# A hybrid token mixer with an MLP behind it: loads of x on another queue, squares in PSUM, and a second norm in fewer steps

## The chip, the cores and the metric

The program runs on one core of a Trainium2 chip. The metric is the device time of one execution in microseconds (us). A core has TensorE (PE, matrix products), VectorE (DVE), ScalarE (ACT), GpSimd (POOL) and SyncE (SP, which here only issues transfers). Each engine works through its own list of instructions in order and waits at the head of that list until the semaphores of the instruction are there. ACT, POOL and SP also issue DMA transfers from their lists.

## The reference

One layer: a mixer of three head groups, an output projection, then a squared-ReLU MLP and a last norm. What the change touches starts at the output projection.

```
def rmsnorm(x, g):
    y = x * lax.rsqrt(jnp.mean(x * x, axis=-1, keepdims=True) + NORM_EPS)
    return y * g
def modulate(x, g, shift, scale):
    return rmsnorm(x, g) * (1 + scale) + shift
def sq_relu_mlp(h, w1, w2):
    return jnp.square(jax.nn.relu(h @ w1)) @ w2

# x (1, 1024, 1024), w_out (1024, 1024), w1 (1024, 4096), w2 (4096, 1024), all float32
x = x + g1 * (concat(hyena, gla, gdn) @ w_out)
x = x + g2 * sq_relu_mlp(modulate(x, norm2_g, sh2, sc2), w1, w2)
out = rmsnorm(x, final_norm_g)
```

## The kernel before

Everything is held transposed: features on the 128 partitions, tokens along the row. x is eight tiles `x1_0` to `x1_7` of 128 features by 1024 tokens. The token axis has two halves, c=0 and c=1.

The nine products behind the mixer (w_out; then four groups of 1024 hidden features, each with a w1 and a w2 product) all go through `stage`. A stage computes a 1024x1024x1024 product as seven products i = 1..7 of 512-blocks (a Strassen scheme) in an order O1, O2 or O3. One product i has four groups p of output features, each with four contraction tiles k and three matmuls (high by high, high by low, low by high: a float32 value is split into two reduced parts, line 292, `split`), so 48 matmuls of 512 columns; a stage has 336. The moving side of product i is four tiles `T` (`sums`, made one product ahead), the stationary side is a tile `S` for each p, cut out of a loaded weight tile `wr0` to `wr3`. ACT makes the high part of both (line 295), DVE the low part of `T` and POOL the low part of `S` (line 255).

Sums of weight blocks are made by the transfers themselves: `weights` loads a block from SP's list (line 1493) and adds others to it by accumulating transfers from POOL's list (line 1487), by the plan of the order (`PLANS`). Four rooms hold five such tiles of a stage in turn.

Products add into eight PSUM banks (`psb`). `take` is called when a group p of a product is done: in w_out and w2 it is `adder`, which adds the bank to x1 (DVE, line 263) and, where a feature tile is then complete, squares it (ACT) and adds the square to `acc` (DVE). In w1 it is `up`, which makes the squared ReLU into tiles `ar`.

`w_out` loads x1 at its start (line 1681). `norm2(c)` runs inside a stage, after a group named by a constant: `NORM_AT = (3, 1)` puts the norm of c=0 behind group p=1 of product i=3 in w_out, `NORM1_AT = (1, 3)` that of c=1 behind p=3 of i=1 in the first w1. `rstd` sums `acc` over features on PE (`ones`), takes the root on ACT and the reciprocal on DVE, and spreads the result over the partitions on PE (`ident`). Then h = x1 * rstd (DVE, for c=0 half of it on POOL) and h * A2 + shift (ACT). For c=1 the first four tiles of h are at last replaced by the difference of second and first half, which the first w1 (order O2) uses.

The text's order is not the lists' order: the framework orders the instructions of each engine by priority (text position, lowered inside `sooner`) and a simulated timeline. Transfers of SP and ACT share eight completion semaphores in turn, so a transfer also waits until the one that had its semaphore before has landed.

Of the kernel before, what the change touches and what calls it, by code (L numbers as in the profile page):

```python
# [184 lines left out]
URGENT = 100000  # L185
# [4 lines left out]
MODN = 2  # L190
ORD0=range(8)
ORD1 = (0, 4, 1, 5, 2, 6, 3, 7)
POOL0 = (4, 5, 6, 7)
POOL1 = ()
FPOOL = ((0, 2, 5), (0, 2, 5))
# [6 lines left out]
LAST_AT = (1, 1)  # L202
NORM_AT = (3, 1)
NORM1_AT = (1, 3)
FINAL_AT = (4, 1)
# [9 lines left out]
class Build:  # L215
# [1292 lines left out]

    def stage(self, src, order, moving, take, after=None, last=None, first=None):

# [22 lines left out]
        for n, i in enumerate(order):  # L1533
            begin_w(n + 2)
            if last and n == 6:

                s = [w(i, p) for p in range(4)]
                for j in range(2):
                    c = slice(256 * j, 256 * j + 256)
                    for p in range(4):  # L1540
                        ps, _ = bank(i, p)
                        for k in range(4):
                            ks = slice(128 * k, 128 * k + 128)
                            self.mm3(ps[:, c], (s[p][:, 0, ks], s[p][:, 1, ks]), (T[i][k][:, 0, c], T[i][k][:, 1, c]), False, k == 3, True)
                        take(i, p, ps, c)
                        if after and j == 0 and (i, p) == after[:2]:
                            after[2]()
                        if (j, p) == LAST_AT:
                            last(slice(0, 256))
                last(c)  # L1550
                break
            for p in range(4):
                s = w(i, p)
                ps, begin = bank(i, p)
                for k in range(4):
                    ks = slice(128 * k, 128 * k + 128)
                    self.mm3(ps, (s[:, 0, ks], s[:, 1, ks]), (T[i][k][:, 0], T[i][k][:, 1]), begin and k == 0, k == 3, not begin)
                take(i, p, ps)
                if p == 3:
                    used(i)  # L1560
                if p == 1 and n < 6:
                    sums(order[n + 1])
                if after and (i, p) == after[:2]:
                    after[2]()
# [49 lines left out]
    def adder(self, gate, acc=None, paired=True):  # L1614
# [6 lines left out]

        def full(m, c, s=slice(0, 512)):
            if acc is not None:
                sq = self.M.tile([128, 512], F32, name="sq", bufs=2) if c in acc else self.M.tile([128, 512], F32, name="acc", bufs=2)
                self.act(sq[:, s], self.x1[m][:, 512 * c:512 * c + 512][:, s], AF.Square)
                if c in acc:
                    self.tt(acc[c][:, s], acc[c][:, s], sq[:, s], ADD)
                else:
                    acc[c] = sq
# [7 lines left out]
        def take(i, p, ps, s=slice(0, 512)):  # L1637
            m, n = p, p + 4
            if i in (1, 2):
                add(ps, m, 0)  # L1640
                if i == 2:
                    full(m, 0)
            elif i == 6:
                add(ps, m, 1)
            elif i == 7:
                add(ps, n, 1)
                later(p)
            elif i == 4:
                add(ps, n, 0, s)
                full(n, 0, s)  # L1650
            elif i == 5:
                if not paired:
                    add(ps, m, 1)
                add(ps, n, 1)
                later(p)
            else:
                add(ps, m, 1, s)
                full(m, 1, s)
        return take
# [15 lines left out]
    def w_out(self):  # L1675
        nc, M = self.nc, self.M

        def load():
            self.x1 = [M.tile([128, L], F32, name=f"x1_{k}") for k in range(8)]
            for m in range(8):  # L1680
                nc.scalar.dma_start(self.x1[m], self.I["xT"][m])
        self.acc = {}
        y = lambda k, c: self.y[k][:, 512 * c:512 * c + 512]
        self.stage(self.I["wout"][0], O3, self.in_place(y, O3), self.adder(16, self.acc, False), (*NORM_AT, lambda: self.norm2(0)), None, load)

    def norm2(self, c):
        if c == 0:
            self.H = [self.HP.tile([128, L], F32, name=f"h{k}") for k in range(8)]
        h = lambda k, c: self.H[k][:, 512 * c:512 * c + 512]
        r = self.rstd(self.acc[c])  # L1690
        rs = self.M.tile([128, 512], F32, name="acc", bufs=2)
        self.nc.scalar.copy(rs, r)
        for k in ORD0 if c == 0 else ORD1:
            pool = k in (POOL0, POOL1)[c]
            self.tt(h(k, c), self.x1[k][:, 512 * c:512 * c + 512], rs if pool else r, MUL, self.nc.gpsimd if pool else None)
            self.act(h(k, c), h(k, c), AF.Identity, bias=self.modT[:, 24 + k, 0:1], scale=self.A2[:, k:k + 1])
        if c:
            for k in range(4):
                self.tt(h(k, 1), h(k + 4, 1), h(k, 1), SUB)

# [16 lines left out]
    def mlp(self):  # L1717
        nc, M, x1 = self.nc, self.M, self.x1
        h = lambda k, c: self.H[k][:, 512 * c:512 * c + 512]
        for g in range(4):  # L1720
# [9 lines left out]
            def up(i, p, ps):  # L1730
# [14 lines left out]
                else:  # L1745
                    o = b[p, 0] if i == 2 else b[p, 1]
                    self.tt(ps, o, ps, ADD)
                    square(o, ps, 1.0)
            self.stage(self.I["w1"][g], order, self.apart(h), up, (*NORM1_AT, lambda: self.norm2(1)) if g == 0 else None)
            acc = {} if g == 3 else None  # L1750
            self.stage(self.I["w2"][g], order, self.in_place(lambda k, c: b[k, c], order), self.adder(40, acc), (*FINAL_AT, lambda: self.final(acc, 1)) if g == 3 else None,
                       (lambda s: self.final(acc, 0, s)) if g == 3 else None)
# [15 lines left out]
```

## Time and profile before

| | |
|---|---|
| time, median of 3 runs | 1692.11 us (1689.56 to 1692.68) |
| the profiled execution's own time | 1693.78 us |
| its span | 1691.9 us |
| mean granted clock of TensorE | 0.938 |
| busy PE / DVE / ACT / POOL | 1525.0 / 1256.2 / 802.1 / 706.6 us |
| start of w_out on PE | 918.41 us |
| chain that ended last, by engine | PE 56%, DVE 23%, DMA 8%, ACT 5%, issue 4%, POOL 2% |

PE is busy 90% of the span, but as an average over stages; what matters is where the other 10% lie and what PE waited for there. In a timeline row the bracket gives the idle time ahead of the row's first instruction and what ended it. ACTq and SPq are an engine's list of transfers to issue.

### The profile page before, as it was taken

To read this page: it belongs to the slowest core of one execution; us is meant where nothing else is said; L and a number is where in the kernel's file an instruction comes from. 1 tells how busy PE (TensorE), PEld (TensorE's weight loads), DVE (VectorE), ACT (ScalarE), POOL (GpSimd) and SP (SyncE) were. 2 spreads that over 40 slices of the span, in tenths; PEclk is the share of its full clock that TensorE was granted. 3 is DMA by queue.
4 is the path that set the end of the run, shared out by engine and by line. 5 is a ranking of instruction groups with operands and counts; after the bars stand their busy time and mean duration, and the time that the engine had idled before them with its cause. 6 is when DMAs were issued, how large, how long until landed. Compare 5 with 4: busy or idle time off the path is not lost.

```text
span 1691.9 us, 26193 instructions
## 1 busy us (share of the span) xinstructions
PE 1525.0 (90%) x10096; PEld 1222.7 (72%) x10096; DVE 1256.2 (74%) x1822; ACT 802.1 (47%) x1468; POOL 706.6 (42%) x512
## 2 busy tenths in 40 slices
PE   7899999989899988569798696998999999999997
PEld 2487877766787766558686585787887887887876
DVE  5954598895575586788977887796688759874986
ACT  5422213225765635445553347553554456445544
POOL 0311141413244211354743554454554655555554
PEclk9899999999999877769899799999999999999998
DMA  8333876847456510335439454255747555664732
GB/s 289 128 106 100 285 277 220 268 156 220 133 178 214 197 53 30 133 111 175 143 112 309 139 143 98 82 132 144 140 139 162 158 122 140 158 163 112 174 75 100
DMA packets 116309, 263.10 MB, mean 156 GB/s; under 512 B 29144, under 2 KB 74632, under 8 KB 101465
## 3 DMA queue, kind: packets, MB, share of 16 engines
q1 hardware_dynamic: 84648, 162.83, 28.2%
q0 software_dynamic: 11824, 74.45, 20.7%
q10 hardware_dynamic: 19712, 24.14, 4.4%
q8 instruction: 80, 1.31, 0.3%
q14 instruction: 45, 0.36, 0.1%
HBM read 219.64 MB, written 41.75 MB: 154 GB/s over the span
## 4 chain that ended last, share of the span: by engine, by line
PE 56%; DVE 23%; DMA 8%; ACT 5%; issue 4%; POOL 2%; ACTq 0%; SPq 0%; POOLq 0%; DVEq 0%
PE psb L227 42%; PE pss L227 8%; DVE lv L255 4%; DVE T L255 3%; DMA wr<-in_w 3%; PE psl L227 2%; DVE hb L255 2%; POOL S L255 1%; PE psi L227 1%; DVE x L263 1%; DVE ar L263 1%; PE psd L227 1%; DVE acc L263 1%; DVE bd L255 1%; DVE acc L255 1%
## 5 line engine op out<-in xcount | busy, mean ns | idle before, releaser
L227 PE MATMUL psb<-T,S 128*128 128x512 f32 (+1 forms) x3072 | 708.0, 392 | 45.1 <-POOL S L255 12.4
L227 PEld LDWEIGHTS psb<-T,S 128*128 128x128 f32 x3072 | 577.3, 191 | 173.9 <-POOL S L255 16.7
L255 POOL TENSOR_TENSOR S<-wr,S 128x512 fp32r<-128x512 f32 x252 | 364.2, 1488 | 296.6 <-ACT S L295 288.2
L295 ACT CAST S<-wr 128x512 fp32r<-128x512 f32 x252 | 154.3, 619 | 174.3 <-PE psb L227 91.0
L227 PE MATMUL psb<-ahi,wh 128*128 128x512 f32 x448 | 184.0, 412 | 6.8 <-DVE acc L263 4.1
L227 PE MATMUL psb<-alo,wh 128*128 128x512 f32 x448 | 182.1, 407 | 0.0
L227 PE MATMUL psb<-ahi,wl 128*128 128x512 f32 x448 | 181.0, 404 | 0.0
L255 POOL TENSOR_TENSOR wl<-ws,wh 128x1024 fp32r<-128x1024 f32 x28 | 71.0, 2537 | 207.7 <-ACT wh L295 141.2
L263 DVE SCALAR_TENSOR_TENSOR acc<-psb,vecs,acc 128x504 f32<-128x504 f32 (+5 forms) x168 | 111.4, 678 | 51.3 <-ACT acc L267 49.0
L255 DVE TENSOR_TENSOR T<-h,T 128x512 fp32r<-128x512 f32 x88 | 94.9, 1107 | 69.1 <-ACT T L295 68.7
L263 DVE SCALAR_TENSOR_TENSOR x<-psb,modT,x 128x512 f32<-128x512 f32 (+1 forms) x148 | 105.0, 726 | 44.2 <-PE psb L227 43.8
L255 DVE TENSOR_TENSOR T<-ar,T 128x512 fp32r<-128x512 f32 x112 | 118.8, 1086 | 10.8 <-ACT T L295 10.8
L227 PEld LDWEIGHTS psb<-ahi,wh 128*128 128x128 f32 x448 | 87.4, 195 | 37.3 <-issue 9.1
L227 PEld LDWEIGHTS psb<-alo,wh 128*128 128x128 f32 x448 | 87.6, 196 | 26.7 <-issue 8.8
L227 PEld LDWEIGHTS psb<-ahi,wl 128*128 128x128 f32 x448 | 87.2, 195 | 22.4 <-issue 5.1
L295 ACT CAST T<-ar 128x512 fp32r<-128x512 f32 x112 | 68.1, 619 | 19.6 <-DVE ar L263 15.0
L1487 POOL DMA_DIRECT2D wr<-in_w x46 | 40.6, 882 | 66.6 <-DMA wr<-in_w 53.0
L295 ACT CAST T<-h 128x512 fp32r<-128x512 f32 x88 | 52.1, 619 | 30.1 <-DMA x<-in_xT 18.9
L255 POOL TENSOR_TENSOR bd<-lv,qT 64x1024 f32<-64x1024 f32 x16 | 49.9, 3125 | 37.5 <-PE pss L227 26.0
L267 ACT ACTIVATE acc<-psb,vecs 128x512 f32<-128x512 f32 (+1 forms) x48 | 31.1, 662 | 63.8 <-PE psb L227 29.8
L267 ACT ACT_TABLE_LOAD x27 | 34.6, 1283 | 37.3 <-DVE acc L263 16.9
L267 ACT ACTIVATE ar<-psb 128x512 f32<-128x512 f32 x48 | 28.7, 598 | 47.4 <-DVE psb L255 42.6
(330 smaller groups left out, 2681.6 us busy)
## 6 DMA issues: line engine op xcount, KB each, us to landing
wr<-in_w POOLq DMA_DIRECT2D x46, 1024.0 KB, 8.1
wr<-in_w SPq DMA_DIRECT2D x40, 1024.0 KB, 5.0
mw<-in_wmod SPq DMA_DIRECT2D x32, 512.0 KB, 5.3
ws<-in_win SPq DMA_DIRECT2D x28, 512.0 KB, 4.1
dft<-in_fw POOLq DMA_DIRECT2D x8, 1024.0 KB, 6.0
dft<-in_iv POOLq DMA_DIRECT2D x8, 1024.0 KB, 7.7
kq<-dKQ SPq DMA_DIRECT2D x64, 96.0 KB, 2.4
wl<-in_wmod SPq DMA_DIRECT2D x8, 512.0 KB, 3.8
```

Source lines behind the costliest of these rows:

```text
L227: return self.nc.tensor.matmul(out, lhsT=lhsT, rhs=rhs, start=start, stop=stop, skip_group_check=more)
L255: return (eng or self.nc.vector).tensor_tensor(out, a, b, op)
L263: return (eng or self.nc.vector).scalar_tensor_tensor(out, a, s, b, op0=op0, op1=op1)
L267: return self.nc.scalar.activation(out, a, f, bias=bias, scale=scale)
L295: self.nc.scalar.copy(hi, src)
L1487: gp.dma_start(tiles[t], src[:, i, j, :], accum_op=ADD)
```

## The change

x1 is loaded from SP's list. A square goes back into the PSUM bank that has just been added to x1 instead of into an SBUF tile, wherever the bank is at hand; the squares made later in `later` stay in SBUF. Both norms are called earlier: `NORM_AT = (3, 0)`, `NORM1_AT = (1, 1)`. The first norm makes all eight tiles on DVE. The second makes x1 * A2 * rstd in one DVE instruction a tile, then the difference tiles from these and from `ds`, a small tile with the differences of the shifts that lies in the MLP's pool, and adds the shift on ACT only to the last four; its DVE work has priority. In the first w1, product i=6 runs with k outside and p inside (`together`). All w2 stages take order O1; the first one had O2.

```
-ORD0=range(8)
-ORD1 = (0, 4, 1, 5, 2, 6, 3, 7)
-POOL0 = (4, 5, 6, 7)
-POOL1 = ()
-NORM_AT = (3, 1)
-NORM1_AT = (1, 3)
+NORM_AT = (3, 0)
+NORM1_AT = (1, 1)
...
+            if i in together:
+                s = [w(i, p) for p in range(4)]
+                b = [bank(i, p) for p in range(4)]
+                for k in range(4):
+                    ks = slice(128 * k, 128 * k + 128)
+                    for p in range(4):
+                        ps, begin = b[p]
+                        self.mm3(ps, (s[p][:, 0, ks], s[p][:, 1, ks]), (T[i][k][:, 0], T[i][k][:, 1]), begin and k == 0, k == 3, not begin)
+                    if k == 1:
+                        sums(order[n + 1])
+                for p in range(4):
+                    take(i, p, b[p][0])
...
-        def full(m, c, s=slice(0, 512)):
+        def full(m, c, s=slice(0, 512), ps=None):
             if acc is not None:
-                sq = self.M.tile([128, 512], F32, name="sq", bufs=2) if c in acc else self.M.tile([128, 512], F32, name="acc", bufs=2)
+                if c not in acc:
+                    sq = self.M.tile([128, 512], F32, name="acc", bufs=2)
+                else:
+                    sq = self.M.tile([128, 512], F32, name="sq", bufs=2) if ps is None else ps
...
-                nc.scalar.dma_start(self.x1[m], self.I["xT"][m])
+                nc.sync.dma_start(self.x1[m], self.I["xT"][m])
...
     def norm2(self, c):
+        h = lambda k, c: self.H[k][:, 512 * c:512 * c + 512]
+        x = lambda k: self.x1[k][:, 512 * c:512 * c + 512]
+        shift = lambda k: self.modT[:, 24 + k, 0:1]
         if c == 0:
             self.H = [self.HP.tile([128, L], F32, name=f"h{k}") for k in range(8)]
-        h = lambda k, c: self.H[k][:, 512 * c:512 * c + 512]
-        r = self.rstd(self.acc[c])
-        rs = self.M.tile([128, 512], F32, name="acc", bufs=2)
-        self.nc.scalar.copy(rs, r)
-        for k in ORD0 if c == 0 else ORD1:
-            pool = k in (POOL0, POOL1)[c]
-            self.tt(h(k, c), self.x1[k][:, 512 * c:512 * c + 512], rs if pool else r, MUL, self.nc.gpsimd if pool else None)
-            self.act(h(k, c), h(k, c), AF.Identity, bias=self.modT[:, 24 + k, 0:1], scale=self.A2[:, k:k + 1])
-        if c:
+            r = self.rstd(self.acc[c])
+            for k in range(8):
+                self.tt(h(k, 0), x(k), r, MUL)
+                self.act(h(k, 0), h(k, 0), AF.Identity, bias=shift(k), scale=self.A2[:, k:k + 1])
+            return
+        ds = self.M.tile([128, 4], F32, name="ds")
+        self.tt(ds, self.modT[:, 28:32, 0], self.modT[:, 24:28, 0], SUB)
+        with self.sooner(URGENT):
+            r = self.rstd(self.acc[c])
             for k in range(4):
-                self.tt(h(k, 1), h(k + 4, 1), h(k, 1), SUB)
+                for i in (k, k + 4):
+                    self.stt(h(i, 1), x(i), self.A2[:, i:i + 1], r, MUL, MUL)
+                self.stt(h(k, 1), h(k + 4, 1), ds[:, k:k + 1], h(k, 1), ADD, SUB)
+        for k in range(4, 8):
+            self.act(h(k, 1), h(k, 1), AF.Identity, bias=shift(k))
...
-            self.stage(self.I["w1"][g], order, self.apart(h), up, (*NORM1_AT, lambda: self.norm2(1)) if g == 0 else None)
+            self.stage(self.I["w1"][g], order, self.apart(h), up, *((*NORM1_AT, lambda: self.norm2(1)), None, None, (6,)) if g == 0 else ())
             acc = {} if g == 3 else None
-            self.stage(self.I["w2"][g], order, self.in_place(lambda k, c: b[k, c], order), self.adder(40, acc), (*FINAL_AT, lambda: self.final(acc, 1)) if g == 3 else None,
+            self.stage(self.I["w2"][g], O1, self.in_place(lambda k, c: b[k, c], O1), self.adder(40, acc), (*FINAL_AT, lambda: self.final(acc, 1)) if g == 3 else None,
```

In the last w2 stage the takes of the last product are also called inside `sooner(URGENT)`.

ACT's list at the start of w_out, before: `T0` to `T3` are the moving tiles of product 1, `T4` to `T7` those of 5, `T8`, `T9`, `T0`, `T1` those of 2, and `h0` to `h7` hold the mixer's output.

```order
L295 CAST T2_8899<-h2_7567 128x512
L1681 DMA x1_0_8905<-in_xT 128x1024
L295 CAST T3_8902<-h3_7568 128x512
L1681 DMA x1_1_8906<-in_xT 128x1024
L1681 DMA x1_2_8907<-in_xT 128x1024
L1681 DMA x1_3_8908<-in_xT 128x1024
L1681 DMA x1_4_8909<-in_xT 128x1024
L1681 DMA x1_5_8910<-in_xT 128x1024
L1681 DMA x1_6_8911<-in_xT 128x1024
L1681 DMA x1_7_8912<-in_xT 128x1024
L295 CAST T9_9051<-h5_7559 128x512
L295 CAST T8_9048<-h4_7569 128x512
```

ACT's list at the same place, after (lines count four lower there):

```order
L291 CAST T2_8899<-h2_7567 128x512
L291 CAST T9_9051<-h5_7559 128x512
L291 CAST T3_8902<-h3_7568 128x512
L291 CAST T8_9048<-h4_7569 128x512
L291 CAST T0_9054<-h6_7560 128x512
L291 CAST T4_8959<-s_8957 128x512
L291 CAST T5_8964<-s_8962 128x512
L291 CAST S_9012<-wr1_8890 128x512
```

The eight loads no longer stand between the casts. SP's list at that place, after; before, `wr2_8921` (the weights of product 2) came straight behind the row of `h3`:

```order
L1344 DMA h3_7568<-dy3_112 128x512
L1699 DMA x1_0_8905<-in_xT 128x1024
L1699 DMA x1_1_8906<-in_xT 128x1024
L1699 DMA x1_2_8907<-in_xT 128x1024
L1699 DMA x1_3_8908<-in_xT 128x1024
L1699 DMA x1_4_8909<-in_xT 128x1024
L1699 DMA x1_5_8910<-in_xT 128x1024
L1699 DMA x1_6_8911<-in_xT 128x1024
L1699 DMA x1_7_8912<-in_xT 128x1024
L1489 DMA wr2_8921<-in_wout 128x2048
L1489 DMA wr3_9193<-in_wout 128x2048
```

The eight loads now stand ahead of the weights of products 2 and 4. DVE's list in the first w1 stage, from the second norm's difference tiles on, before: `u` is made from `h0` to `h3` for product 6, and the `psb` rows are takes of product 2.

```order
L255 TENSOR_TENSOR h7_9501<-x1_7_8912,psb_9686 128x512
L255 TENSOR_TENSOR psb_9716<-ar_9609,psb_9716 128x512
L255 TENSOR_TENSOR h0_9494<-h4_9498,h0_9494 128x512
L255 TENSOR_TENSOR psb_9735<-ar_9627,psb_9735 128x512
L255 TENSOR_TENSOR h1_9495<-h5_9499,h1_9495 128x512
L255 TENSOR_TENSOR psb_9774<-ar_9657,psb_9774 128x512
L255 TENSOR_TENSOR h2_9496<-h6_9500,h2_9496 128x512
L263 SCALAR_TENSOR_TENSOR u_9751<-h0_9494 128x512
L263 SCALAR_TENSOR_TENSOR u_9756<-h1_9495 128x512
L255 TENSOR_TENSOR h3_9497<-h7_9501,h3_9497 128x512
```

DVE's list at the same place, after:

```order
L259 SCALAR_TENSOR_TENSOR h7_9473<-x1_7_8912,A2_67,psb_9638 128x512
L259 SCALAR_TENSOR_TENSOR h0_9466<-h4_9470,ds_9628,h0_9466 128x512
L259 SCALAR_TENSOR_TENSOR h1_9467<-h5_9471,ds_9628,h1_9467 128x512
L259 SCALAR_TENSOR_TENSOR h2_9468<-h6_9472,ds_9628,h2_9468 128x512
L259 SCALAR_TENSOR_TENSOR h3_9469<-h7_9473,ds_9628,h3_9469 128x512
L259 SCALAR_TENSOR_TENSOR u_9734<-h0_9466 128x512
L259 SCALAR_TENSOR_TENSOR u_9739<-h1_9467 128x512
L251 TENSOR_TENSOR T0_9830<-h0_9466,T0_9830 128x512
L259 SCALAR_TENSOR_TENSOR u_9744<-h2_9468 128x512
L259 SCALAR_TENSOR_TENSOR u_9749<-h3_9469 128x512
```

The difference tiles follow the norm without takes between them and without a step on ACT.

## Rows read from the trace of the kernel before

**Rows 1.** Stretches from w_out: length, busy PE PEld DVE ACT POOL (count), clock, DMA, GB/s
```profile
930.20:959.20 29.00, 15.05 (x48) 10.97 (x49) 24.09 (x34) 11.86 (x22) 13.65 (x7) 0.71 0.53 171
959.20:1008.90 49.70, 49.61 (x217) 40.50 (x218) 42.08 (x47) 23.75 (x41) 27.49 (x21) 1.00 0.43 109
1008.90:1029.20 20.30, 14.79 (x65) 11.44 (x63) 16.52 (x15) 12.22 (x21) 11.28 (x10) 0.92 0.39 98
1029.20:1060.00 30.80, 20.43 (x94) 16.43 (x95) 23.72 (x36) 22.17 (x40) 12.84 (x11) 0.88 0.66 137
1060.00:1108.00 48.00, 48.00 (x207) 39.55 (x207) 37.33 (x44) 29.13 (x53) 24.00 (x17) 0.97 0.30 87
1108.00:1156.00 48.00, 43.23 (x184) 35.36 (x183) 47.27 (x52) 20.33 (x35) 26.77 (x20) 0.95 0.65 154
1156.00:1264.00 108.00, 108.00 (x473) 89.08 (x471) 70.77 (x82) 52.87 (x94) 57.74 (x45) 0.99 0.56 137
```

**Rows 2.** Timeline of PE and ACT, start of w_out: start, us, engine, line, what
```profile
915.99 18.42 ACTq L1681 DMA_DIRECT2D x<-in_xT  x6
918.41 11.79 PE L227 MATMUL psb<-T,S 128*128 128x512 f32 x48
...
934.46 1.66 ACT L295 CAST T<-h 128x512 fp32r<-128x512 f32 x3 [18.94 <-DMA x<-in_xT]
...
938.83 2.28 PE L227 MATMUL psb<-T,S 128*128 128x512 f32 x4 [8.63 <-ACT S L295]
```

**Rows 3.** Stretches 915 to 941, columns as in rows 1
```profile
915.00:925.00 10.00, 8.90 (x36) 6.85 (x37) 5.90 (x13) 0.52 (x1) 0.00 (x0) 0.78 1.03 260
925.00:941.00 16.00, 7.37 (x27) 5.08 (x26) 5.89 (x10) 4.98 (x9) 2.14 (x1) 0.75 0.92 369
```

**Rows 4.** Transfers issued from 915 to 920: size, median us to landing
```profile
wr<-in_wout SPq DMA_DIRECT2D x2, 1024.0 KB, 17.9
```

**Rows 5.** The chain that ended last, 918 to 934
```profile
918.83 14.66 DMA wr<-in_wout
```

**Rows 6.** Timeline of all engines at the first norm
```profile
1008.88 0.95 PE L227 MATMUL psb<-ones,acc 128*128 128x1 f32 x8
...
1010.68 7.66 DVE L255 TENSOR_TENSOR acc<-acc,sq 128x512 f32<-128x512 f32 x1 [0.34 <-ACT sq L267]
1011.31 5.72 PE L227 MATMUL psb<-T,S 128*128 128x512 f32 x24
...
1012.50 5.27 POOL L255 TENSOR_TENSOR h<-x,acc 128x512 f32<-128x512 f32 x4
...
1021.75 7.19 PE L227 MATMUL psb<-T,S 128*128 128x512 f32 x23 [4.73 <-ACT T L295]
```

**Rows 7.** Groups of DVE instructions, 918 to 1030: count, busy, mean ns, idle before
```profile
L255 DVE TENSOR_TENSOR T<-h,T 128x512 fp32r<-128x512 f32 x29 | 30.1, 1056 | 16.4 <-ACT T L295 16.4
L263 DVE SCALAR_TENSOR_TENSOR x<-psb,modT,x 128x512 f32<-128x512 f32 x32 | 23.0, 740 | 0.8 <-PE psb L227 0.5
L255 DVE TENSOR_TENSOR acc<-acc,sq 128x512 f32<-128x512 f32 x14 | 19.2, 1372 | 7.4 <-ACT sq L267 7.4
```

**Rows 8.** Timeline at the second norm
```profile
1039.38 4.87 DVE L255 TENSOR_TENSOR h<-x,psb 128x512 f32<-128x512 f32 x8 [5.67 <-ACT acc L1692]
...
1051.67 1.36 PE L227 MATMUL psb<-T,S 128*128 128x512 f32 x4 [3.78 <-ACT T L295]
...
1059.62 15.58 PE L227 MATMUL psb<-T,S 128*128 128x512 f32 x61 [6.59 <-DVE T L255]
```

**Rows 9.** Timeline in the first w2 stage
```profile
1140.10 7.89 DVE L255 TENSOR_TENSOR T<-ar,T 128x512 fp32r<-128x512 f32 x2
...
1152.28 12.89 PE L227 MATMUL psb<-T,S 128*128 128x512 f32 x43 [4.77 <-DVE x L263]
```

**Rows 10.** Squares: ACT and DVE, 918 to 1030, ns min/median/max
```profile
L267 ACT ACTIVATE sq<-x x14: 617/632/634, 969.1 to 1028.3; 128x512 f32<-128x512 f32 x14
L255 DVE TENSOR_TENSOR acc<-acc,sq x14: 679/693/7660, 969.8 to 1029.0; 128x512 f32<-128x512 f32 x14
```

More of the change, by code (lines that the diff above doesn't have):

```diff
@@ L1507, in weights, with stage @@
         return get, begin, lambda i: further(at[i])
-    def stage(self, src, order, moving, take, after=None, last=None, first=None):
+    def stage(self, src, order, moving, take, after=None, last=None, first=None, together=()):
         w, begin_w, used = self.weights(src, order)
@@ L1544, in stage @@
                             self.mm3(ps[:, c], (s[p][:, 0, ks], s[p][:, 1, ks]), (T[i][k][:, 0, c], T[i][k][:, 1, c]), False, k == 3, True)
-                        take(i, p, ps, c)
+                        with self.sooner(URGENT):
+                            take(i, p, ps, c)
                         if after and j == 0 and (i, p) == after[:2]:
@@ L1548, in stage @@
                         if (j, p) == LAST_AT:
-                            last(slice(0, 256))
+                            with self.sooner(URGENT):
+                                last(slice(0, 256))
                 last(c)
                 break
+            if i in together:
[10 more added lines that the diff above has]
+                    take(i, p, b[p][0])
+                    if after and (i, p) == after[:2]:
+                        after[2]()
+                used(i)
+                continue
             for p in range(4):
@@ L1641, in take @@
                 if i == 2:
-                    full(m, 0)
+                    full(m, 0, s, ps)
             elif i == 6:
@@ L1649, in take @@
                 add(ps, n, 0, s)
-                full(n, 0, s)
+                full(n, 0, s, ps)
             elif i == 5:
@@ L1657, in take @@
                 add(ps, m, 1, s)
-                full(m, 1, s)
+                full(m, 1, s, ps)
         return take
@@ L1686, in norm2 @@
     def norm2(self, c):
+        h = lambda k, c: self.H[k][:, 512 * c:512 * c + 512]
+        x = lambda k: self.x1[k][:, 512 * c:512 * c + 512]
+        shift = lambda k: self.modT[:, 24 + k, 0:1]
         if c == 0:
             self.H = [self.HP.tile([128, L], F32, name=f"h{k}") for k in range(8)]
-        h = lambda k, c: self.H[k][:, 512 * c:512 * c + 512]
-        r = self.rstd(self.acc[c])
-        rs = self.M.tile([128, 512], F32, name="acc", bufs=2)
-        self.nc.scalar.copy(rs, r)
-        for k in ORD0 if c == 0 else ORD1:
-            pool = k in (POOL0, POOL1)[c]
-            self.tt(h(k, c), self.x1[k][:, 512 * c:512 * c + 512], rs if pool else r, MUL, self.nc.gpsimd if pool else None)
-            self.act(h(k, c), h(k, c), AF.Identity, bias=self.modT[:, 24 + k, 0:1], scale=self.A2[:, k:k + 1])
-        if c:
-            for k in range(4):
-                self.tt(h(k, 1), h(k + 4, 1), h(k, 1), SUB)
+            r = self.rstd(self.acc[c])
[5 more added lines that the diff above has]
+        self.tt(ds, self.modT[:, 28:32, 0], self.modT[:, 24:28, 0], SUB)
+        with self.sooner(URGENT):
+            r = self.rstd(self.acc[c])
+            for k in range(4):
+                for i in (k, k + 4):
[3 more added lines that the diff above has]
+            self.act(h(k, 1), h(k, 1), AF.Identity, bias=shift(k))
     def final(self, acc, c, s=slice(0, 512)):
```

## The prediction, made before the changed kernel ran

> **What bounds the kernel now.** I first cut the span into stretches [rows 1]. From 1156 to 1264 us PE is busy all the time at a clock of 0.99 and does 473 matmuls in 108.0 us, 0.228 us each: that is full speed here, 10.9 us for a product of 48. Four earlier stretches fall behind it, and what PE waited for in them says whose waits can go.
>
> - 930.2 to 959.2 (product 5 of w_out): 48 matmuls in 29.0 us, 18.1 us more than 10.9, at a clock of 0.71. The timeline [rows 2] shows why: PE ends product 1 at 930.2 and then waits 8.63 us for `S` from ACT; ACT stood idle for 18.94 us up to 934.46, because its next casts are queued behind the eight loads of x, and the last six of those took 18.42 us to be issued. The seventh load waits for the semaphore that the weights of product 2 hold; these took 14.66 us to land [rows 5]. DVE and POOL then start on what ACT left, and PE gets its operands one by one, at half clock.
> - 959.2 to 1008.9: 217 matmuls in 49.7 us, 0.229 each. Nothing lost, though DVE is busy for 42.1 of it [rows 1].
> - 1008.9 to 1029.2 (first norm): 24 + 23 wide matmuls [rows 6] are worth 10.7 us, the sums for the norm take 2.4 us (1008.88 to 1011.31), so 7.2 of 20.3 us are lost. On DVE one add `acc<-acc,sq` takes 7.66 us, through the 5.27 us in which POOL makes four tiles of h; PE idles 4.73 us and comes back slow.
> - 1029.2 to 1060 (second norm): 94 instructions, 16 of them the norm's small ones; 78 x 0.228 = 17.8, and 1.8 for the small ones, leave 11.2 of 30.8 us lost. PE waits 3.78 and 6.59 us for `T` [rows 8].
> - 1108 to 1156 (end of the first w1, start of its w2): 184 x 0.228 = 42.0, so 6.0 of 48 us lost. DVE is busy for 47.3 of 48 [rows 1]; two low parts take 7.89 us and PE waits 4.77 us for an add to x1 [rows 9].
>
> **The change part by part.**
>
> *Loads of x on SP.* ACT loses the eight issues and with them the 18.94 us. What comes next for product 5? Its `S` needs ACT and POOL, its `T4` to `T7` need DVE's differences; both engines are nearly free between 920 and 934 (ACT is busy for 0.52 us from 915 to 925 [rows 3]), so these are made while PE runs product 1, and PE goes on at 930.2. The loads don't get shorter: DMA is busy at 0.92 to 1.03 up to 941 [rows 3]. SP now issues the 4 MB of x ahead of the 2 MB of weights for products 2 and 4, each of which took 17.9 us to land [rows 4]. In total bytes all is there by 941 as before; with x first, I put the weights of product 2, last but one in the list, at 938 (941 less 1 MB at 369 GB/s). PE wants them at 930.2 + 10.9 = 941.1. Cast and subtraction take about 2 us, so that holds, but ACT's list has three casts for later products in front that wait until PE has read its last `T4` and `T5`; about 2 us are then lost ahead of product 2, and I add 2.5 us for adds to x1 that wait for their load and for a DVE that has its work in fewer microseconds. So 13.6 of the 18.1 us go. Bounds: 18.1 at best; at worst, only ACT's issue time (8 x 0.34 us, say 2.7), if the transfers are what PE waits for.
>
> The Trainium skill's page "DMA: Bandwidth & Descriptors", section "Issuing engines are not separate DMA queues", says that starting DMAs from several engines saves only the time to start them, which is small. By it alone this edit is worth the 2.7 us above. The trace agrees that all of them share one set of DMA engines (share near 1.0), but also has the 18.94 us of ACT, which is a wait at the head of a list and not transfer time. I make the rule a rival.
>
> *Squares into PSUM.* 25 of 32 squares change place. Their ACT step costs 0.63 us [rows 10]; with a PSUM output no row has it, and I take the same, between 0.5 and 0.8. The DVE add goes from 1.372 us on average (0.693 in the median, 7.66 at most [rows 7, 10]) to what an instruction with one PSUM and one SBUF input takes, 0.74 at most [rows 7]: 11 of the 14 adds of w_out change, 11 x 0.63 = 6.9 us of DVE, none of it on PE's path except the 7.66 us, counted with the norm. A bank is held longer, by 0.63 + 0.69 = 1.3 us plus DVE's queue; I take this as hidden, since the next product's four banks are other ones (a rival below prices it).
>
> The skill's page "SBUF — State Buffer", section "Who interferes with whom", says that a DVE instruction with two SBUF inputs is blocked by a GpSimd one that reads SBUF, and one with at most one SBUF input is not. Rows 7 agree: 1056 and 1372 ns with two, 740 ns with one. By the rule the four tiles of h that POOL made would no longer block anything either.
>
> *First norm.* One group earlier, so three groups (36 x 0.228 = 8.2 us) instead of two run on PE while it is made. DVE now makes eight tiles (8 in 4.87 us [rows 8]), one add of 0.74 and the low part 0.69, 6.3 us from the end of the sums on; that is inside 8.2 us. ACT's eight steps and the casts run beside it. I keep 1.0 of the 7.2 us for the other tiles: 6.2 gained. Bounds 0 and 7.2.
>
> *Second norm.* Eight fused instructions (0.74 each at most, by the row of another instruction with three inputs [rows 7]) and four differences come without ACT's step and without takes between. It starts two groups earlier (2 x 2.7 us), so from the end of the sums PE has 24 + 48 matmuls, 16.4 us. DVE needs 8 x 0.7 + 4 x 0.65 = 8.2 us, then five instructions up to the first `u` tiles' low parts and four of these, 6 to 8 us with takes between: 14 to 16 us. That just fits, and `together` needs the four tiles only one after the other. The sums themselves can wait on `acc`, which DVE finishes only behind six casts' low parts: up to 2 us. I keep 4.0 of 11.2 us: 7.2 gained. Bounds: 0 (DVE late as before) and 11.2, and 0.8 more from the clock after it (207 in 48.0 us [rows 1]).
>
> *O1 in the first w2.* Product 5, second in O1, needs the first half less the second, which comes from the last product of w1; in O2 that was wanted third. From the last matmul to `T` are six steps of 0.6 to 0.7, about 4 us, against 10.9 of product 1. DVE is full here, so I take nothing gained: between 6.0 (the wait goes) and -8 (a blocked pair of 7.89 us [rows 9] lands in this path). O1 also adds one 1 MB accumulating transfer, hidden behind two products.
>
> *The end.* Its lists are the same but for the banks of the squares: 0, between 1 and -1.
>
> Sum: 13.6 + 6.2 + 7.2 + 0 = 27.0. The profiled execution took 1693.8 us, 1.7 above the median of the runs; 1693.8 - 27.0 = 1666.8, as a median 1665.1 us.
>
> **The rivals.**
>
> - *The wait moves to DVE.* From 930 to 1156 it is busy for 191 of 226 us (rows 1 added up); with 27 us less span, 6.9 us of blocked adds less and four tiles more it would be at 94%, in order. Then the adds free the banks late and PE waits there, as it does for 4.77 us in rows 9. About half stays: 8 + 4 + 2 = 14, 1678 us. Against it: full speed at 42.1 of 49.7 us of DVE [rows 1], where the first half of this work lies.
> - *The transfers are the bound.* By the page's rule the loads end at 941 in any case; if the weights of product 2 land behind that, the first term is 2.7: 2.7 + 6.2 + 7.2 = 16.1, 1676.0 us. For it: 17.9 us to landing. Against it: PE has work of its own up to 941.
> - *All of it goes,* the wait in the first w2 too: 17 + 7.2 + 12 + 6 = 42, 1650 us.
> - *Slower: squares hold the banks.* Each of the 25 keeps its bank 1.3 us longer. If PE needs just this bank next, 25 x 1.32 = 33 us are added and 27.0 go: 1698. It decides from 27.0 / 25 = 1.08 us a square on. Against it: only the last adds of the kernel are waited for by PE now, and eight banks serve products of four.
> - *It doesn't do what it says:* x waits on SP for its room until the mixer's end, near 918, and all behind it too. The weights of product 2 had that same wait before, so this costs little and falls under the second rival.
>
> **How the numbers follow.** Likeliest 0.56 (own range 1656 to 1673); DVE 0.22; transfers 0.08; all 0.10; slower 0.04. The range from 1650 to 1680 takes in the second and third and most of the fourth. Within 0.2% (3.4 us) can't be told from no change: 0.02; faster 0.95, slower 0.03.
>
> **What would show it.** Right: ACT has no wait for x; PE's product 5 starts within 2 us of the end of 1, and w_out's 264 matmuls up to the first norm take about 64 us instead of 79; no DVE add of several us at the first norm; PE waits under 4 us in all around the second. Wrong: PE waits for `wr` ahead of product 2, or for DVE in front of each product at a full DVE; a wait of 8 us or more in the first w2; PE waiting for adds to `acc`.

## The result

The changed kernel takes 1666.96 us in the median of four executions (1665.6 to 1673.8); the kernel before, measured beside it, takes 1692.39 (1689.6 to 1695.4). These two medians lie 25.4 us apart, a quotient of 0.985. The ratio on record, with a 95% interval, is 0.9881 (0.9851 to 0.9911); by it the kernel is faster by some 20 us, 15 to 25. The ratios below are of this kind, each against runs of the kernel before on the same chip. A second set of runs of the unaltered changed kernel (E11 below) gave 0.9881 again (0.9853 to 0.9908). Predicted were 1665.1 us.

The profiled execution took 1667.06 us, its span is 1665.3. From the page of the profile: busy time of each engine, and the chain that ended last.

```profile
PE 1516.9 (91%) x10096; PEld 1217.1 (73%) x10096; DVE 1264.2 (76%) x1827; ACT 797.1 (48%) x1462; POOL 704.3 (42%) x509
PE 60%; DVE 18%; DMA 9%; issue 5%; ACT 5%; POOL 3%; ACTq 0%; POOLq 0%; SPq 0%; DVEq 0%
```

The timeline of the changed kernel, PE and the queue of SP (start, length, engine, line, what, count, and in brackets the idle time before with what ended it; lines count four lower than before):

```profile
906.45 15.29 SPq L1699 DMA_DIRECT2D x<-in_xT  x8
913.94 18.40 PE L223 MATMUL psb<-T,S 128*128 128x512 f32 x76
935.10 6.45 PE L223 MATMUL psb<-T,S 128*128 128x512 f32 x20 [2.76 <-DVE T L251]
941.77 46.61 PE L223 MATMUL psb<-T,S 128*128 128x512 f32 x204 [0.22 <-DVE x L259]
988.22 0.95 PE L223 MATMUL psb<-ones,acc 128*128 128x1 f32 x8
990.64 13.87 PE L223 MATMUL psb<-T,S 128*128 128x512 f32 x60
1005.94 1.02 PE L223 MATMUL psb<-ones,acc 128*128 128x1 f32 x8 [1.42 <-DVE acc L251]
1008.83 20.99 PE L223 MATMUL psb<-T,S 128*128 128x512 f32 x86
1030.56 8.00 PE L223 MATMUL psb<-T,S 128*128 128x512 f32 x34 [0.73 <-POOL S L251]
1040.12 0.73 PE L223 MATMUL psb<-T,S 128*128 128x512 f32 x2 [1.57 <-ACT S L291]
1041.58 57.43 PE L223 MATMUL psb<-T,S 128*128 128x512 f32 x245 [0.72 <-POOL S L251]
1101.95 2.60 PE L223 MATMUL psb<-T,S 128*128 128x512 f32 x10 [2.94 <-DVE T L251]
1106.11 13.22 PE L223 MATMUL psb<-T,S 128*128 128x512 f32 x57 [1.55 <-DVE T L251]
1121.43 5.76 PE L223 MATMUL psb<-T,S 128*128 128x512 f32 x24 [2.10 <-POOL S L251]
```

Read it against [rows 2, 6, 8, 9]. Product 1 runs into product 5 without a gap (76 matmuls in a row instead of 48 and a wait of 8.63 us); a wait of 2.76 us comes later in product 5. From its start at 925.8 to the norm's sums 252 matmuls take 62.4 us, as 264 would take 65.1, for the 64 forecast. The first norm's sums stand at 988.22, and 60 wide matmuls follow with no stall, where the kernel before idled 4.73 us. The second norm's waits of 3.78 and 6.59 us are gone; in their place stand 1.42 us for an add to `acc` (the norm's sums) and small ones for `S`. In the first w2 there are new waits for low parts. The eight issues of x still take 15.29 us on SP's list, but nothing that makes operands stands behind them there.

**A part of the gain is not the change's.** PE starts w_out at 913.94 us, 4.5 us earlier than before [rows 2], though no edit touches the mixer; what differs ahead of w_out is only who issues x, from 906.45 us on. The traces place the difference earlier: counted by PE's matmuls, the changed kernel is 6.8 us ahead where the kernel before stands at 650 us, and 4.7 at 864 us, before the first load of x. Fourteen profiled executions of this study, none with an edit in the mixer, start w_out between 911.6 and 924.1; one and the same kernel did so at 916.6 and at 920.1 (E4 and E12 below), the changed kernel at 913.9 and 914.6, which by itself would decide nothing. So from w_out on the change gives 773.5 - 751.3 = 22.2 us of the 26.6 by which the two spans differ.

That makes a finer measure than the whole time: each trace holds all 3072 wide matmuls of w_out and the MLP, and I take the time from the start of the first to the moment when n are done with and the next starts. The table gives the lead: by how many us a kernel is sooner there than the kernel before. 288 are six products of w_out, 384 are w_out and product 1 of the first w1 (the first norm lies in between, and the sums of the second), 528 reach to the end of its products 6 and 7, which wait for the second norm, and 1008 to the end of the first w2; "end" is the end of the span.

| kernel | ratio to before, 95% | w_out at | 288 | 384 | 528 | 1008 | end |
|---|---|---|---|---|---|---|---|
| changed | 0.9881 (0.9851-0.9911) | 913.9 | 13.5 | 16.7 | 23.9 | 23.3 | 22.2 |
| E11 changed, again | 0.9881 (0.9853-0.9908) | 914.6 | 13.5 | 16.8 | 24.1 | 20.3 | 22.7 |
| E1 before + x on SP | 0.9906 (0.9869-0.9942) | 914.7 | 13.5 | 19.1 | 19.2 | 19.4 | 20.6 |
| E2 changed, x on ACT | 0.9943 (0.9921-0.9965) | 918.0 | -0.1 | 3.1 | 12.9 | 12.6 | 14.2 |
| E6 before + squares in PSUM | 0.9973 (0.9953-0.9993) | 920.7 | 1.8 | 7.8 | 7.4 | 8.9 | 9.2 |
| E3 changed, squares in SBUF | 0.9943 (0.9915-0.9971) | 924.1 | 13.5 | 10.6 | 17.3 | 13.2 | 16.2 |
| E5 changed, POOL makes h4-h7 | 0.9876 (0.9837-0.9914) | 915.1 | 11.7 | 13.3 | 22.3 | 18.6 | 19.9 |
| E7 changed, old second norm | 0.9906 (0.9872-0.9940) | 922.9 | 13.5 | 19.9 | 20.9 | 18.3 | 18.8 |
| E8 changed, wr2 after x3 | 0.9887 (0.9848-0.9926) | 911.6 | 13.5 | 16.7 | 23.8 | 22.9 | 25.6 |
| E9 changed, no interleaving | 0.9878 (0.9853-0.9903) | 915.9 | 13.5 | 16.7 | 28.4 | 23.4 | 24.0 |
| E4 changed, O2 | 0.9854 (0.9825-0.9884) | 916.6 | 13.5 | 16.9 | 24.2 | 25.7 | 26.9 |
| E12 the same, again | 0.9880 (0.9851-0.9910) | 920.1 | 13.8 | 16.9 | 25.0 | 25.5 | 27.7 |
| E10 O2, no interleaving | 0.9883 (0.9857-0.9909) | 913.0 | 13.5 | 16.9 | 28.7 | 26.9 | 25.1 |

Up to 528 the changed kernel's two executions and E8, whose lists differ from it in one place of SP's alone, agree within 0.3 us; at 1008 they spread over 3 us and at the end over 3.4.

### The profile page after: what moved, and what is told of

Its sections match the earlier page's. It is cut to its first block, busy times and chain, and to the rows that moved or that the text cites. A ratio compares the mean times of both kernels' runs of the same rounds, so it can differ in the third digit from the quotient of the medians.

```text
span 1665.3 us, 26163 instructions
## 1 busy us (share of the span) xinstructions
PE 1516.9 (91%) x10096; PEld 1217.1 (73%) x10096; DVE 1264.2 (76%) x1827; ACT 797.1 (48%) x1462; POOL 704.3 (42%) x509
## 4 chain that ended last, share of the span: by engine, by line
PE 60%; DVE 18%; DMA 9%; issue 5%; ACT 5%; POOL 3%; ACTq 0%; POOLq 0%; SPq 0%; DVEq 0%
PE psb L223 45%; PE pss L223 8%; DMA wr<-in_w 5%; DVE lv L251 4%; POOL S L251 2%; PE psl L223 2%; DVE T L251 2%; DVE hb L251 2%; PE psi L223 1%; PE psd L223 1%; DVE bd L251 1%; DMA alo<-in_xT 1%; DVE acc L259 1%; ACT acc L263 1%; DMA dvt<-acc 1%
## 5 line engine op out<-in xcount | busy, mean ns | idle before, releaser
L223 PE MATMUL psb<-T,S 128*128 128x512 f32 (+1 forms) x3072 | 702.6, 390 | 25.7 <-POOL S L251 12.6
L223 PEld LDWEIGHTS psb<-T,S 128*128 128x128 f32 x3072 | 574.0, 190 | 152.9 <-POOL S L251 18.6
L251 DVE TENSOR_TENSOR T<-ar,T 128x512 fp32r<-128x512 f32 x112 | 130.3, 1189 | 15.9 <-ACT T L291 15.9
L223 PEld LDWEIGHTS psb<-ahi,wl 128*128 128x128 f32 x448 | 87.1, 194 | 22.3 <-issue 5.1
L1483 POOL DMA_DIRECT2D wr<-in_w x47 | 41.7, 888 | 80.8 <-DMA wr<-in_w 71.7
L263 ACT ACTIVATE ar<-psb 128x512 f32<-128x512 f32 x48 | 28.7, 599 | 52.8 <-DVE psb L251 48.1
L263 ACT ACT_TABLE_LOAD x27 | 34.6, 1283 | 38.6 <-DVE acc L259 18.6
```

The source lines that it names most:

```text
L223: return self.nc.tensor.matmul(out, lhsT=lhsT, rhs=rhs, start=start, stop=stop, skip_group_check=more)
L251: return (eng or self.nc.vector).tensor_tensor(out, a, b, op)
L263: return self.nc.scalar.activation(out, a, f, bias=bias, scale=scale)
L1483: gp.dma_start(tiles[t], src[:, i, j, :], accum_op=ADD)
```

## The experiments

### E1, E2: who issues x

E1 is the kernel before with

```
-                nc.scalar.dma_start(self.x1[m], self.I["xT"][m])
+                nc.sync.dma_start(self.x1[m], self.I["xT"][m])
```

> The kernel before, with one line changed: the eight loads of x are issued by SP instead of ACT. Theory of the prediction (they block ACT's list): 13.6 us less than before, some 1679 us; PE's product 5 starts within 3 us of the end of product 1, ACT has no wait of 18 us, and the stall at the first norm (add of 7.66 us) stays. Rival, transfers are the bound: only ACT's issue time goes, 2.7 us, some 1690 us, and PE waits for the weights of product 2 instead. Rival, the wait moves to DVE: about 8 us, 1684 us, with waits of PE for DVE's adds up to 1108 us.

Its timeline of PE, DVE and POOL:

```profile
914.71 18.46 PE L227 MATMUL psb<-T,S 128*128 128x512 f32 x76
935.82 6.45 PE L227 MATMUL psb<-T,S 128*128 128x512 f32 x20 [2.65 <-DVE T L255]
942.48 49.35 PE L227 MATMUL psb<-T,S 128*128 128x512 f32 x216 [0.22 <-DVE x L263]
992.15 2.80 POOL L255 TENSOR_TENSOR S<-wr,S 128x512 fp32r<-128x512 f32 x2
993.47 2.04 DVE L255 TENSOR_TENSOR acc<-acc,sq 128x512 f32<-128x512 f32 x1 [0.34 <-ACT sq L267]
995.04 5.85 POOL L255 TENSOR_TENSOR h<-x,acc 128x512 f32<-128x512 f32 x4
1028.87 1.63 PE L227 MATMUL psb<-T,S 128*128 128x512 f32 x4 [3.78 <-ACT T L295]
1036.82 87.76 PE L227 MATMUL psb<-T,S 128*128 128x512 f32 x380 [6.32 <-DVE T L255]
```

The first three rows match those of the changed kernel up to the 288th matmul: 13.5 us, by this one line. What no theory expected is the first norm: the add `acc<-acc,sq` took 2.04 us instead of 7.66, and another 5.6 us came (19.1 at 384), though nothing in the norm was edited. The second norm's 3.78 and 6.32 us stayed. The time, 0.9906, is 15.9 us less with an interval of 9.8 to 22.1, which holds both the 13.6 expected and the 19 to 21 of the trace: only the trace tells them apart.

E2 is the line put back in the changed kernel (`nc.sync` to `nc.scalar`).

> The changed kernel with its loads of x back on ACT. If the loads on SP are worth 13.6 us by themselves: 1667 + 13.6 = 1680.6 us, with ACT's wait of some 18 us and the wait of PE in product 5 back. If they are worth only the time to issue them: 1669.7 us. If the edits depend on each other (the norm starts a group earlier and so needs DVE sooner), more than 13.6: over 1683 us.

Its PE timeline has the old stall again:

```profile
917.99 12.36 PE L223 MATMUL psb<-T,S 128*128 128x512 f32 x48
937.51 2.29 PE L223 MATMUL psb<-T,S 128*128 128x512 f32 x4 [7.17 <-ACT S L291]
943.49 12.29 PE L223 MATMUL psb<-T,S 128*128 128x512 f32 x44 [3.70 <-POOL S L251]
```

13.6 us are lost at 288, 11.0 at 528 and 8.0 at the end of the span; by the ratios it is some 10. The rival of the issue time alone (2.7 us) is out on both sides.

### E6, E3, E5: squares, POOL and the first norm

E6 is the kernel before with 25 squares in PSUM, and E3 the changed kernel with `sq` in SBUF:

```
E6: -        sq = (...) if c in acc else self.M.tile([128, 512], F32, name="acc", bufs=2)
    +        sq = (...) if c not in acc else self.M.tile([128, 512], F32, name="sq", bufs=2) if ps is None else ps
    -        full(m, 0)
    +        full(m, 0, s, ps)
E3: -        sq = self.M.tile([128, 512], F32, name="sq", bufs=2) if ps is None else ps
    +        sq = self.M.tile([128, 512], F32, name="sq", bufs=2)
```

> The kernel before with 25 of its 32 squares written to PSUM, and nothing else changed; POOL still makes four tiles of h in the first norm. If a DVE add with one input in SBUF is not held up by POOL: the add of 7.66 us is 0.7 us long, the mean of these adds goes from 1.37 to 0.7 us, and up to 4.7 us of PE's wait go: 1688 to 1692 us. If the long add comes from POOL whatever its inputs are: the 7.66 us stay, 1692 us. If the squares hold banks that PE needs: slower than before, in the end up to 33 us, with PE waiting for adds to acc all through w_out and the last w2.

> The changed kernel with its squares in SBUF again. POOL makes no tile of h any more. Theory of the prediction: the adds to acc are 0.7 us where POOL is idle and longer beside its subtractions, some 7 us more of DVE in w_out, nearly all hidden: 1667 to 1670 us. If the squares in PSUM carry the gain at the norms (a full DVE): 1672 us or more. If they hold banks PE waits for: less than 1667 us.

E5 is the changed kernel with

```
-                self.tt(h(k, 0), x(k), r, MUL)
+                self.tt(h(k, 0), x(k), rs if k > 3 else r, MUL, self.nc.gpsimd if k > 3 else None)
```

where `rs` is a copy of `r` in SBUF.

> The changed kernel with the first norm's tiles h4 to h7 made by POOL again (from a copy of the row of factors in SBUF, as before), squares still in PSUM. If what POOL blocks is a DVE instruction with two SBUF inputs: the adds to acc stay near 0.7 us, but a low part T (two SBUF inputs) that stands beside POOL's 5 us grows to several us; PE waits 0 to 5 us: 1667 to 1672 us. If squares in PSUM alone had ended it: 1667 us and no DVE instruction over 2 us. If POOL blocks any DVE instruction: an add to acc of 5 us or more, 1672 us.

In each the place of POOL's four `h` tiles in the timeline, or for E3 the second norm's sums. In the kernel before, POOL's work just ahead of its `h` tiles [rows 6]:

```profile
1010.02 2.81 POOL L255 TENSOR_TENSOR S<-wr,S 128x512 fp32r<-128x512 f32 x2
```

E6:

```profile
1011.18 0.69 DVE L255 TENSOR_TENSOR acc<-acc,psb 128x512 f32<-128x512 f32 x1 [0.31 <-ACT psb L267]
1012.78 5.52 POOL L255 TENSOR_TENSOR h<-x,acc 128x512 f32<-128x512 f32 x4
```

E5:

```profile
992.93 0.69 DVE L251 TENSOR_TENSOR acc<-acc,psb 128x512 f32<-128x512 f32 x1 [0.31 <-ACT psb L263]
995.45 5.33 POOL L251 TENSOR_TENSOR h<-x,acc 128x512 f32<-128x512 f32 x4
999.15 3.44 DVE L251 TENSOR_TENSOR T<-h,T 128x512 fp32r<-128x512 f32 x1 [1.52 <-ACT T L291]
1000.48 1.55 POOL L251 TENSOR_TENSOR S<-wr,S 128x512 fp32r<-128x512 f32 x1
```

E3:

```profile
1016.21 3.40 POOL L251 TENSOR_TENSOR S<-wr,S 128x512 fp32r<-128x512 f32 x2
1018.42 1.74 DVE L251 TENSOR_TENSOR acc<-acc,sq 128x512 f32<-128x512 f32 x1
1020.21 1.86 PE L223 MATMUL psb<-ones,acc 128*128 128x1 f32 x8 [5.26 <-DVE acc L251]
```

With [rows 6] this is one picture. A DVE instruction with two SBUF inputs that is issued while POOL works ends some 0.56 us after the end of one of POOL's instructions, four times over: at 1018.34 in the kernel before (POOL's `h` up to 1017.77), 995.51 in E1 (`S` up to 994.95), 1002.59 in E5 (`S` up to 1002.03, behind `h`) and 1020.16 in E3 (1019.61). It is no chance of four: from 900 us on, the fourteen traces have 1539 DVE adds and subtractions of two SBUF tiles of 512 columns (low parts, differences, adds to `acc`) that take 0.9 us or more, and each ends 0.54 to 0.56 us after the end of one of POOL's. Which one it is decides the length. Where DVE got its turn, POOL's next instruction starts at most 0.07 us before the end of the one it follows, or later; at the 187 ends through which DVE stayed held, the next one had started 0.10 to 0.37 us before that end. In the kernel before, `h` starts at 1012.50 while `S` runs up to 1012.83, and the `h` tiles overlap in the same way: 7.66 us. In E1 `h` starts 0.09 us after `S` has ended: 2.04 us. (These are the profile's spans, which are rough on POOL.) With one input in PSUM the add takes 0.69 us (E6, E5): of 1228 DVE instructions with a PSUM input that stand beside POOL's work in these traces, none takes over 0.85. In E5 the next instruction with two in SBUF, a low part `T`, pays 3.44 us instead. The Trainium skill (page "SBUF — State Buffer", section "Who interferes with whom") states this division by the number of SBUF inputs; these rows agree.

E6 gives 6.0 us at the first norm (1.8 to 7.8), more than the 4.7 expected, and shows no new wait for banks. E3 loses 6.6 us by 528, not up to 3: the adds to `acc` are late, and PE waits 5.26 us for the second norm's sums; its ratio, 0.9943, lies clear of the changed kernel's. E5 loses 1.8 us already ahead of the norm, where nothing was edited but the tiles (a wait for `S`), and 1.6 more at it; by 528 it is 1.6 behind, and its ratio, 0.9876, shows no loss.

### E7, E9: the second norm and its interleaved product

E7 puts back the old second norm (eight products with ACT's step behind each, then the differences), its old place and no interleaving; E9 takes only the interleaving away:

```
E7: -NORM1_AT = (1, 1)
    +NORM1_AT = (1, 3)
    -                    self.stt(h(i, 1), x(i), self.A2[:, i:i + 1], r, MUL, MUL)
    +            self.tt(h(k, 1), x(k), r, MUL)
    +            self.act(h(k, 1), h(k, 1), AF.Identity, bias=shift(k), scale=self.A2[:, k:k + 1])
E9: -... None, None, (6,)) if g == 0 else ()
    +... None, None, ()) if g == 0 else ()
```

> The changed kernel with the second norm as before: two groups later, eight products on DVE each followed by ACT's scale and shift, then four differences, and product 6 of the first w1 not interleaved. Theory of the prediction: 7.2 us of the second norm's 11.2 come back: 1674 us, with PE waits of 3.8 and 6.6 us for low parts in front of product 6. If DVE's relief by the squares in PSUM had done it: 1667 us and no such waits.

> The changed kernel with product 6 of the first w1 not interleaved (its four groups one after the other), all else kept; the fused second norm, its place and O1 stay. If interleaving is what the second norm's gain rests on: the first group of product 6 waits for its four tiles, some 3 to 6 us lost between the 384th and 528th matmul of w_out, as with the old second norm (118.9 us there became 116.5). If the low parts that stand beside POOL's subtractions set the pace in both: within 1 us of the changed kernel's 38.1 us for that stretch.

(The figures in the bracket of the last text, 118.9 and 116.5, are a slip: the stretch from 384 to 528 took 45.3 us before and 44.3 in E7.) E7 has a wait of 5.95 us for `T` again, in front of product 6:

```profile
1035.44 0.50 PE L223 MATMUL psb<-T,S 128*128 128x512 f32 x1 [2.25 <-ACT S L291]
1041.89 69.25 PE L223 MATMUL psb<-T,S 128*128 128x512 f32 x291 [5.95 <-DVE T L251]
```

At 528 it is 2.9 to 3.2 us behind the changed kernel (its two executions), not the 7.2 forecast. E9 is 4.5 us *ahead* of the changed kernel there: both expectations missed, the interleaving costs. Against E7, the fused norm two groups earlier without interleaving is worth 7.5 us (28.4 less 20.9), close to the 7.2 forecast. None of E9's 4.5 us is left at 1008, and its ratio, 0.9878, is that of the changed kernel. Timeline of E9 at product 6:

```profile
1032.43 64.08 PE L223 MATMUL psb<-T,S 128*128 128x512 f32 x281 [0.63 <-POOL S L251]
1038.34 6.93 POOL L251 TENSOR_TENSOR S<-wr,S 128x512 fp32r<-128x512 f32 x4 [2.30 <-ACT S L291]
```

and of the changed kernel:

```profile
1037.25 0.62 ACT L291 CAST T<-s 128x512 fp32r<-128x512 f32 x1 [1.87 <-PE psb L223]
1038.45 0.62 ACT L291 CAST T<-s 128x512 fp32r<-128x512 f32 x1 [0.58 <-DVE s L259]
1039.45 0.62 ACT L291 CAST S<-wr 128x512 fp32r<-128x512 f32 x1
1040.16 1.36 POOL L251 TENSOR_TENSOR S<-wr,S 128x512 fp32r<-128x512 f32 x1 [6.00 <-ACT S L291]
```

In the changed kernel POOL is idle for 6.00 us for want of a cast, and PE waits 1.57 and 0.72 us for that `S` (rows at 1040.12 and 1041.58 above). In E9 POOL goes on after 2.30 us, and PE runs 281 matmuls in a row. Two reasons can be read from code and rows, and no run parts them. `S` has four buffers: four groups done one after the other give them back one by one, four interleaved groups hold all four until their last round, which here ends for the first group at 1036.4 us (39 of product 6's 48 matmuls). And the cast of `S` comes only at 1039.45, because ACT's list has two casts of `T` in front of it that wait for other engines until 1037.25 and 1038.45; in E9 no `T` stands there. That interleaving costs is shown; whether by the buffers or by the order of ACT's list stays open, since neither a fifth buffer nor another order was tried.

### E8: weights of product 2 sooner

```
             begin_w(n + 2)
+            if first and n == 0:
+                first(range(4, 8))
```

where `first()` loads x0 to x3 as before.

> The changed kernel with the weights of product 2 issued on SP between the fourth and the fifth tile of x instead of behind the eighth. If transfers were a bound (weights of product 2 late): up to 2 us less, 1665 us. If only DVE's adds to x wait for data in this stage: x4 to x7 land some 3 us later, the second PE wait in product 5 grows from 2.8 us, and the time is 1667 to 1670 us. If neither is on PE's path: 1667 us.

The same lead to 0.1 us up to 528: neither the weights nor the last tiles of x are on PE's path. What PE waits 2.76 us for in product 5 is DVE itself, by the changed kernel's busy times in the first of two stretches (length, then PE, PEld, DVE, ACT, POOL with counts, clock, DMA, GB/s):

```profile
926.00:940.00 14.00, 11.24 (x42) 8.78 (x42) 13.86 (x20) 4.14 (x8) 4.35 (x4) 0.88 0.97 323
1028.80:1060.00 31.20, 28.18 (x115) 22.22 (x114) 30.06 (x30) 16.37 (x32) 19.40 (x14) 0.95 0.52 119
```

DVE is busy for 13.86 of 14 us. The second stretch, around product 6 of the first w1, is used further below.

### E11, E12, E4, E10: O1 or O2 in the first w2

E4 and E12 are one kernel, the changed one with

```
-self.stage(self.I["w2"][g], O1, self.in_place(lambda k, c: b[k, c], O1), ...
+self.stage(self.I["w2"][g], order, self.in_place(lambda k, c: b[k, c], order), ...
```

E11 is the changed kernel unaltered, E10 has this edit and E9's.

> The changed kernel with the old order of products (O2) in the first w2, all else kept. Prediction's term for this edit: 0, so 1667 us. In the changed kernel PE waits 7.2 us in this stage for low parts and S; if O1 is what makes these waits (product 5 second, which needs the last product of w1), O2 is faster by up to 4 us: 1663. If DVE's load makes them in either order: waits of 5 to 8 us stay and the time is 1667.

> The changed kernel once more, unaltered, on the chip of the next three runs. From its own profile and the others: PE's first matmul of w_out comes anywhere between 911 and 925 us, since ten profiled executions with the same instructions in front of it show that spread; from there to the 528th matmul 139.8 us and to the 1008th 257 us, each within 1 us. If the 4.5 us by which w_out started earlier in the changed kernel were its own doing, the start lies within 1 us of 913.9.

> The changed kernel with O2 in the first w2, once more, beside the changed kernel on the same chip. If O1 costs what PE's progress in one profile of each says: from the 720th matmul of w_out on to the 1008th some 71.7 us against 73.7, and 2 to 4 us less in all, a time 0.1 to 0.25% below the changed kernel's. If that was chance: no difference of 1 us in this stretch.

> The changed kernel with O2 in the first w2 and without the interleaving: the sum of the two edits. If they are independent: the loss of the one and the gain of the other (2 us in the first w2) add up. If neither changes anything: the time of the changed kernel, ratio near 0.987.

From matmul 528 to 1008 the eight kernels with O1 lose 0.3 to 5.0 us of their lead (2.6 in the mean), and the five with O2 (E4, E12, E10, and E1 and E6, which keep the old stage) between -1.5 and 1.8 (-0.4). From 720 to 1008 it is 71.7 and 72.8 us (E4, E12) against 73.7 and 77.0 (changed, E11; for E11 the expectation of 257 us at the 1008th missed by 3). Over all traces the six with O2 (the kernel before is one) take 71.7 to 75.0 us there, the eight with O1 73.5 to 78.2: some 3 us in the mean, with ranges that overlap. At the end of the span O2 (E4, E12) is 4.9 us ahead, mean of two against mean of two, or 1.7 against E8; E10 is 1.1 ahead of E9. The times don't show it: 0.9854 and 0.9880 against 0.9881 twice, each inside the others' intervals. So the traces speak for O2, by 1 to 5 us, and a faster kernel than the changed one is not shown. In E4 the wait of the kernel before for an add to x1 [rows 9] is back, with the same 4.77 us; O1 trades it for the shorter waits seen above.

```profile
1126.28 73.92 PE L223 MATMUL psb<-T,S 128*128 128x512 f32 x319 [4.77 <-DVE x L259]
```

E10 adds E9's gain at 528; at the end it is some 2 us behind E4 and E12.

## Why the prediction held, and where it did not

- *x on SP, 13.6 us: right.* 13.5 by E1, 13.6 by E2, both at 288. The 4.6 us that stay were put down to the weights of product 2 (2) and to DVE (2.5). PE waits for no weights there: 2.76 us are for a low part and 0.22 us for an add to x1, both DVE's, full in that stretch, and the 20 matmuls behind the first wait take 6.45 us, 0.32 each. The rival of the transfers is out by E1 and E8. (The prediction gives each of two weight transfers 17.9 us to land; one took 14.66 by [rows 5]. Nothing hangs on it.) The Trainium skill's rule that the prediction quotes (page "DMA: Bandwidth & Descriptors", section "Issuing engines are not separate DMA queues": only the time to start transfers is saved) does not cover a list that stands still: the measurement decides, 13.5 against 2.7.
- *Squares in PSUM, nothing on the path but the 7.66 us: too low.* The add fell to 0.683 us, within what was worked out (0.74 at most; 11 adds, 1.372 before). But "none of it on PE's path" failed: E3 shows 6.6 us there by 528, because the second norm's sums, two groups earlier, now wait for the last of these adds. The banks were no price: PE's waits for `acc` are 4.8 us in all from w_out on, 3.4 of them at the kernel's end, where the kernel before waits 3.4 too, and 1.42 at the second norm's sums, for which the prediction had allowed 2. Its reading that POOL's tiles "would no longer block anything" was too wide: a low part `T` still has two SBUF inputs and took 3.44 us in E5. PE's waits in the changed kernel (total us, times, longest):

```profile
PE psb L223 <- DVE T L251: 7.3, 3, 2.9
PE psb L223 <- DVE acc L251: 4.8, 2, 3.4
PE psb L223 <- ACT S L291: 4.0, 3, 2.3
```

- *First norm, 6.2 us: the size right, the reason too narrow.* E7, which has the changed first norm and the old second one, gains 6.4 us between 288 and 384. But the stall goes by either of two edits alone: the loads on SP (5.6 in E1, where POOL's `h` came to start just behind `S`) or the squares (6.0 in E6). No run has the norm without POOL's tiles as its only edit. I added the norm as a term of its own; in E1 it is already in the first.
- *Second norm, 7.2 us: too high.* Both norms together gave 23.9 - 13.5 = 10.4 us by 528, where 13.4 was forecast. The step that failed is the help expected from interleaving, "`together` needs the four tiles only one after the other": it asks for the moving tiles one by one, but holds four `S` tiles to the end, and with it the stretch takes 4.5 us more (E9). Without it the two norms give 14.9 by 528, and the second by itself 7.5 against E7: the rest of the term was sized right.
- *O1, 0 us between +6.0 and -8: the bounds held.* From 528 to 1008 the two executions of the changed kernel lose 0.5 and 3.8 us against the kernel before.
- *The sum.* 27.0 was forecast from w_out on, 22.2 and 22.7 were measured, and the time's own interval says 15 to 25. That the forecast time came out 1.9 us from the median is luck: of the 26.7 us between the two profiled executions, 4.5 arose in the mixer ahead of w_out, which the change does not touch. The mechanism and the first term were right; the second norm was mis-sized by the interleaving.
- *The rival "the wait moves to DVE"* holds in product 5 and in part of the first w2, where PE's new waits are for low parts. It does not hold at product 6: there DVE is busy for 30.06 of 31.20 us in the changed kernel, but in E9 for 31.11, and PE does 136 matmuls instead of 115:

```profile
1028.80:1060.00 31.20, 30.57 (x136) 24.98 (x135) 31.11 (x31) 19.08 (x37) 22.87 (x15) 1.00 0.54 132
```

E9's 4.5 us at 528 are given back by 1008 (5.0), with PE waits of 3.60 us for a low part and 2.19 for `S` in the first w2. That DVE's load takes back there what is won before it fits these rows, and no run shows it by itself.

## What to carry to other kernels

A transfer that must wait for a semaphore should not be issued from the list of an engine that has operands to make. That one line gave 13.5 us where it acts; in E1's trace it gave 20.6 of the 22 us by the end, 5.6 of them because two instructions of POOL happened not to overlap, and putting the line back in the changed kernel costs 8.0 by the end (E2). Where several edits meet at one stall, each of them may remove it, so their gains don't add: try each alone. And interleaving groups is not free: it asks for one operand later and holds every buffer of the other to the end, and here it cost 4.5 us at its own place.

## What the runs showed that was not expected

- Whether POOL holds up a DVE instruction with two SBUF inputs for 7.66 or for 2.04 us was decided by 0.4 us in the start of one instruction of POOL: 0.33 before the end of the one ahead of it, or 0.09 behind. A trace of one alignment doesn't price such a stall.
- Fourteen executions reach w_out within a range of 12.5 us (911.6 to 924.1) with the same mixer ahead of it; the 288 matmuls that follow repeat to 0.1 us in nine of the eleven that load x on SP. Counted from a common instruction, repeats of one kernel agree within 1 us up to the 528th matmul (E11 with the changed kernel, E12 with E4), where the whole time doesn't tell 5. By the 1008th, two executions of the changed kernel are 3 us apart again.
